# A planner that counts the exclusion of VectorE and GpSimd on SBUF, in a two-layer decoder trunk

## The chip, the core and the metric

The kernel runs on one NeuronCore of a Trainium2 chip. Five engines work side by side, each through its own instructions in order: TensorE (PE, matrix products; PEld in the profile is its weight loading), VectorE (DVE), ScalarE (ACT), GpSimd (POOL) and SyncE (SP, which here starts all DMA transfers). They wait for each other through semaphores. The metric is the device time of one execution in microseconds; the time before is the median of three runs, 1509.18 us (1507.07 to 1511.28).

## The reference

A decoder trunk of two layers on 512 tokens of width 1024, in float32. In each layer:

```
h = rmsnorm(x, g_pre_mix);  proj = h @ w_in          # split into queries, keys, values of four head groups
o_a = top-k sparse attention (an indexer scores the keys, 128 are kept per token)
o_b = forgetting attention (logits plus differences of cumulated log gates)
o_c = differential attention (probs[:, 0] - lam * probs[:, 1], then a norm)
o_d = sliding-window attention with sinks
x = x + rmsnorm(concat(o_a, o_b, o_c, o_d) @ w_out, g_post_mix)
h = rmsnorm(x, g_pre_mlp)
x = x + rmsnorm(square(relu(h @ w_up)) @ w_down, g_post_mlp)      # inner width 4096
x = x + sigmoid(x @ w_ple_gate) * (p_i @ w_ple_proj)
```

Queries and keys of groups a, c and d and of the indexer are rotated (rope).

## The kernel before, in words

Each large product is made of three products of float32r halves: a value is split into a high half (a rounded copy) and a low half (the value less the high half), and `mm3` (line 466) sums high x high, high x low and low x high in PSUM. So every weight tile of 128x1024 that SP loads (`wload`, line 448) costs a copy `whi` on ACT or DVE and a subtraction `wlo` on DVE or POOL, and every activation tile costs a copy (`hth`, or an R, V or P tile) and a subtraction (`htl` and the like). A layer goes through the norm and the rope tables, the head tiles (`head_tile`, line 628: a projection, evacuated from one of two `ps_mm` banks by DVE, rotated by products with the `tab` tiles), the values, the indexer and its top-k (`topk`, line 765, all on DVE), the four attentions, the split of their outputs (`mix_split`, line 779, tiles O), the output projection, 32 tiles of the MLP's first product and four groups of its second, and the gate. `add_normed` (line 526) adds a normed half to x: R<-P,ss,R on DVE, after a small power on POOL. Attention c (line 880) combines two probability tiles on DVE: Z<-Z,s,Z.

The program is not issued as it is written. Class `Plan` records every instruction with its reads and writes, `schedule` (line 290) plays the whole program through once with a cost for each instruction (`price`, line 246) and a table of delays between engines (`SEEN`, line 113), and `emit` (line 417, with line 429 the one line of nearly all rows of the profile) issues the instructions in the order of the planned start times. That order is the program of each engine, and also settles which tile takes which buffer. At each step the engine with the earliest possible start takes the ready instruction of smallest `prio`, which is the place in the written program plus a shift of its step.

Some instructions are recorded with two forms (`either`, line 166): `wlo`, the splits of SBUF tiles, the rope products, the products with a gain, and the copies to a high half. For these `sooner_elsewhere` (line 399) compares the engines: for each, the start it could have, plus the cost of the ready fixed instructions ahead of it, plus the instruction's cost there, plus a bias on DVE. The bias is set by step (lines 1248 to 1261): 4000 ns for v1 and aqk, 2500 for dq, bqk and cqk, 2000 for the output projection, 1500 for va and vc, 1000 for d, 600 for the gains at the start, iq, topk, mix and b, 500 for the MLP, 300 for ik, dk and a, 0 for index and c. If the other engine is better, the form of this one is dropped for good.

In `price`, a DVE instruction of n columns costs n x 1.0417 + 69 ns (n x 0.52 + 69 for a copy, tensor_scalar or memset not read from PSUM, and 61 more with a per-partition operand or a second operation), and a two-input one on POOL n x 2.1 + 147. No cost depends on what the other engine is doing.

Of the kernel before, what the change touches and what calls it, by code (L numbers as in the profile page):

```python
# [134 lines left out]
class Plan:  # L135
# [110 lines left out]
    def price(self, eng, fn, a, k, outs, ins):  # L246
# [25 lines left out]
            return (470.0 if k.get("op") == ALU.pow else n * 2.1 + 147), 0.0  # L272
        return n * 0.833 + 244, 0.0

    @contextmanager
    def after(self, i):

        old, self.held = self.held, i
        yield
        self.held = old  # L280
# [9 lines left out]
    def schedule(self):  # L290
        ops = self.ops
        for i, o in enumerate(ops):
            o.left, o.open = len(o.deps), dict(o.alts) if o.alts else None
            for d in o.deps:
                ops[d].succ.append(i)
            for e in o.alts or (o.eng,):
                o.ready[e] = 0.0
        engines = ("PE", "DVE", "ACT", "POOL", "SP")
        now = dict.fromkeys(engines, 0.0)
        future = {e: [] for e in engines}  # L300
        avail = {e: [] for e in engines}
        dma, now["SP"] = 0.0, 560.0
        table = None
        waiting, live, last, queue = {}, {}, {}, {}

        def push(i):
            for e, r in ops[i].ready.items():
                heapq.heappush(future[e], (r, ops[i].prio, i))

        def after(q, eng, end):  # L310
            for e, r in q.ready.items():
                q.ready[e] = max(r, end if eng == e == "ACT" else end + SEEN[eng, e])

        def grant(t, slot):
            t.granted, t.slot = True, slot
            for i in waiting.pop(t, ()):
                o = ops[i]
                o.left -= 1
                for eng, end in t.freed:
                    after(o, eng, end)  # L320
                if o.left == 0:
                    push(i)

        for tag, (bufs, pool, tiles) in self.tags.items():
            queue[tag] = list(reversed([t for t in tiles if t.ops]))
        for o in ops:
            for t in o.tiles:
                t.granted = t.tag is None or t.tag == "dram"
                t.freed, t.ends = (), {}
        for i, o in enumerate(ops):  # L330
            for t in o.tiles:
                if not t.granted:
                    waiting.setdefault(t, []).append(i)
                    o.left += 1
            if o.left == 0:
                push(i)
        for tag, (bufs, pool, tiles) in self.tags.items():
            for slot in range(bufs):
                if queue[tag]:
                    grant(queue[tag].pop(), slot)  # L340
        order = []
        while True:
            best = None
            for e in engines:
                f, v = future[e], avail[e]
                while f and (f[0][0] <= now[e] or ops[f[0][2]].done):
                    _, p, i = heapq.heappop(f)
                    heapq.heappush(v, (p, i))
                while v and ops[v[0][1]].done:
                    heapq.heappop(v)  # L350
                s = now[e] if v else f[0][0] if f else None
                if s is not None and (best is None or s < best[0]):
                    best = (s, e)
            if best is None:
                break
            s, e = best
            now[e] = max(now[e], s)
            f, v = future[e], avail[e]
            while f and f[0][0] <= s:
                _, p, i = heapq.heappop(f)  # L360
                heapq.heappush(v, (p, i))
            _, i = heapq.heappop(v)
            o = ops[i]
            if o.done or self.sooner_elsewhere(o, e, s, now, avail):
                continue
            o.start, o.done = s, True
            if o.alts:
                o.eng = e
                o.fn, o.a, o.k, o.cost, o.size = o.open[e]
            cost = o.cost  # L370
            if e == "PE" and s < COLD:
                cost *= 2
            if e == "ACT" and o.table and o.table != table:
                cost, table = cost + 1283, o.table
            now[e] = s + cost
            if e == "SP":
                dma = max(dma, s + cost + 650) + o.size
                o.end = dma
            else:
                o.end = now[e]  # L380
            order.append(i)
            for j in o.succ:
                q = ops[j]
                q.left -= 1
                after(q, e, o.end)
                if q.left == 0:
                    push(j)
            for t in o.tiles:
                t.ops -= 1
                t.ends[e] = max(t.ends.get(e, 0.0), o.end)  # L390
                if t.ops == 0 and t.tag is not None and t.tag != "dram" and queue[t.tag]:
                    n = queue[t.tag].pop()
                    n.freed = tuple(t.ends.items())
                    grant(n, t.slot)
        assert len(order) == len(ops), f"{len(ops) - len(order)} instructions never became ready"
        self.total = max(o.end for o in ops)
        return order

    def sooner_elsewhere(self, o, e, s, now, avail):
        if not o.open or len(o.open) < 2:  # L400
            return False
        best = None
        for g, c in o.open.items():
            t = s if g == e else max(now[g], o.ready[g])
            if g != e:
                t += sum(self.ops[i].cost for p, i in avail[g] if p < o.prio and not self.ops[i].done
                         and not self.ops[i].alts)
            t += c[3] + o.bias.get(g, 0.0)
            if best is None or t < best[0]:
                best = (t, g)  # L410
        if best[1] != e:
            del o.open[e]
            del o.ready[e]
            return True
        return False
# [952 lines left out]
```

## Time and profile before

| | |
|---|---|
| median of three runs | 1509.18 us (1507.07 to 1511.28) |
| the profiled execution | 1507.25 us, its span 1505.5 us |
| TensorE's granted clock over the span | 0.987 of full speed |
| instructions in the span | 19889 |
| busy: PE, DVE, ACT, POOL | 1445.8, 908.8, 661.1, 376.7 us |
| HBM read and written | 127.38 and 5.24 MB |

The span is from the first to the last instruction of the profiled execution. A group of rows gives its form as out<-in with buffer numbers left out, the number of instructions, their busy time in us, the mean in ns, and the idle time of the engine before them with what ended it. Matmuls overlap, so a PE that is busy is not necessarily at its peak. An instruction on DVE is counted from its start to the end of its last write, and the next one may start some 0.1 us before that.

### The profile page before, as it was taken

How to read it: one execution, taken by the hardware profiler on the slowest of the kernel's cores; microseconds unless marked ns; L12 is line 12 of the kernel's file. 1: busy time of each engine (PE TensorE's matmuls, PEld its weight loads, DVE VectorE, ACT ScalarE, POOL GpSimd, SP SyncE). 2: the span in 40 equal slices, each digit the busy share in tenths (PEclk: the TensorE clock that was granted, in tenths of full speed). 3: DMA queues.
4: the chain of work that ended last, by engine and by line, in shares of the span. 5: the costliest groups of instructions: out<-in, count | busy, mean ns of one | idle time of the engine just before them, and what ended most of it. 6: DMA issues, size and time to landing. Idle time of an engine off the chain costs nothing. (4 is left out here: it accounts for less than half of the span.)

```text
span 1505.5 us, 19889 instructions
## 1 busy us (share of the span) xinstructions
PE 1445.8 (96%) x7476; PEld 1173.3 (78%) x7476; DVE 908.8 (60%) x1789; ACT 661.1 (44%) x1299; POOL 376.7 (25%) x291
## 2 busy tenths in 40 slices
PE   6999998999999999999999999889999999999998
PEld 6967776778888888887789678577788888888877
DVE  7689998756424333335666999986553243433463
ACT  4266656745323223233344665666543341322321
POOL 5564556342000000002145636563310000000020
PEclk8899999999999999999999999999999999999999
DMA  4321122223222222221332211123132222222221
GB/s 160 100 86 57 57 78 98 78 84 112 99 90 93 98 98 88 94 98 56 122 118 71 74 55 64 64 64 120 52 131 98 99 88 94 98 98 90 92 77 63
DMA packets 44624, 133.91 MB, mean 89 GB/s; under 512 B 6896, under 2 KB 8176, under 8 KB 44528
## 3 DMA queue, kind: packets, MB, share of 16 engines
q1 hardware_dynamic: 44528, 132.64, 26.7%
q8 instruction: 59, 0.97, 0.3%
q14 instruction: 37, 0.30, 0.1%
HBM read 127.38 MB, written 5.24 MB: 88 GB/s over the span
## 5 line engine op out<-in xcount | busy, mean ns | idle before, releaser
L429 DVE TENSOR_TENSOR wlo<-wst,whi 128x1024 fp32r<-128x1024 f32 x150 | 184.2, 1228 | 355.6 <-ACT whi L429 355.4
L429 ACT ACTIVATE whi<-wst 128x1024 fp32r<-128x1024 f32 (+1 forms) x212 | 222.7, 1051 | 397.0 <-PE ps_tp L429 202.1
L429 POOL TENSOR_TENSOR wlo<-wst,whi 128x1024 fp32r<-128x1024 f32 (+1 forms) x70 | 168.5, 2410 | 164.2 <-ACT whi L429 155.8
L429 PE MATMUL ps_sc<-htl,whi 128*128 128x512 f32 (+1 forms) x544 | 208.5, 384 | 1.1 <-DVE htl L429 1.1
L429 PE MATMUL ps_sc<-hth,whi 128*128 128x512 f32 (+1 forms) x544 | 207.6, 383 | 0.3 <-ACT hth L429 0.3
L429 PE MATMUL ps_sc<-hth,wlo 128*128 128x512 f32 (+1 forms) x544 | 206.5, 380 | 0.0
L429 POOL TENSOR_SCALAR ss<-ss,eps 128x1 f32<-128x1 f32 x8 | 3.7, 473 | 637.1 <-ACT Z L429 637.1
L429 PE MATMUL ps_mm<-hth,whi 128*128 128x512 f32 (+1 forms) x400 | 148.3, 372 | 9.6 <-DVE R L429 9.2
L429 PE MATMUL ps_mm<-htl,whi 128*128 128x512 f32 (+1 forms) x400 | 148.1, 371 | 1.8 <-DVE htl L429 1.8
L429 PE MATMUL ps_mm<-hth,wlo 128*128 128x512 f32 (+1 forms) x400 | 146.2, 366 | 0.0
L429 PE MATMUL ps_mm<-whi,htl 128*128 128x512 f32 (+2 forms) x344 | 121.1, 353 | 5.6 <-DVE htl L429 5.6
L429 PE MATMUL ps_mm<-whi,hth 128*128 128x512 f32 (+2 forms) x344 | 122.0, 355 | 0.3 <-DVE V L429 0.2
L429 PE MATMUL ps_mm<-wlo,hth 128*128 128x512 f32 (+2 forms) x344 | 120.1, 350 | 0.1
L429 PEld LDWEIGHTS ps_sc<-hth,whi 128*128 128x128 f32 x544 | 102.0, 188 | 23.0 <-ACT hth L429 0.5
L429 PEld LDWEIGHTS ps_sc<-htl,whi 128*128 128x128 f32 x544 | 102.2, 188 | 22.4 <-DVE htl L429 1.5
L429 PEld LDWEIGHTS ps_sc<-hth,wlo 128*128 128x128 f32 x544 | 102.3, 188 | 21.9
L429 ACT ACTIVATE Z<-Z,m 128x256 f32<-128x256 f32 (+3 forms) x160 | 86.2, 541 | 39.4 <-DVE m L429 38.7
L429 PE MATMUL ps_tp<-whi,V 128*128 128x512 f32 x256 | 96.4, 394 | 0.0
L429 PE MATMUL ps_mm<-whi,V 128*128 128x512 f32 x256 | 96.4, 394 | 0.0
L429 PEld LDWEIGHTS ps_mm<-hth,whi 128*128 128x128 f32 x400 | 77.8, 195 | 20.6 <-issue 11.5
L429 POOL TENSOR_TENSOR R<-R,R 128x512 fp32r<-128x512 f32 (+1 forms) x58 | 76.6, 1321 | 59.1 <-ACT R L429 46.0
L429 PEld LDWEIGHTS ps_mm<-htl,whi 128*128 128x128 f32 x400 | 78.0, 195 | 13.1 <-issue 3.0
(213 smaller groups left out, 2957.4 us busy)
## 6 DMA issues: line engine op xcount, KB each, us to landing
wst<-in_wu SPq DMA_DIRECT2D x64, 512.0 KB, 3.2
wst<-in_wd SPq DMA_DIRECT2D x64, 512.0 KB, 3.2
wst<-in_wq SPq DMA_DIRECT2D x40, 512.0 KB, 3.5
wst<-in_wo SPq DMA_DIRECT2D x16, 512.0 KB, 3.3
wst<-in_wg SPq DMA_DIRECT2D x16, 512.0 KB, 3.2
R<-in_x SPq DMA_DIRECT2D x16, 256.0 KB, 3.6
Z<-in_g SPq DMA_DIRECT2D x16, 256.0 KB, 3.6
wst<-in_wv SPq DMA_DIRECT2D x8, 512.0 KB, 3.2
```

The source lines that it names most:

```text
L429: r = getattr(getattr(nc, eng), fn)(*[res(v) for v in o.a], **{n: res(v) for n, v in o.k.items()})
```

## The change

The planner gets a notion of one shared port between DVE and POOL. A new method `shared` says which DVE instructions take it: those whose operands all lie in SBUF and that either read two tiles of more than 64 columns or are a `tensor_copy` or `tensor_scalar`. Every POOL instruction takes it. `schedule` keeps the time at which the port comes free from either engine; a DVE instruction that takes the port is lengthened by what is left of POOL's, and a POOL instruction by what is left of DVE's. `sooner_elsewhere` gets the same times, and puts the possible start on POOL, or on DVE for an instruction that takes the port, no earlier than the other engine's end. Instructions, costs, biases, shifts and buffers stay as they are.

```diff
+    def shared(self, fn, a):
+
+
+        ins = [v for v in a[1:] if isinstance(v, View) and v.free() > 64]
+        if any(self.psum(v) for v in a if isinstance(v, View)):
+            return False
+        return len(ins) > 1 or fn[1] in ("tensor_copy", "tensor_scalar")
...
+        port = {"DVE": 0.0, "POOL": 0.0}
...
-            if o.done or self.sooner_elsewhere(o, e, s, now, avail):
+            if o.done or self.sooner_elsewhere(o, e, s, now, avail, port):
                 continue
...
             if e == "ACT" and o.table and o.table != table:
                 cost, table = cost + 1283, o.table
+            if e == "DVE" and self.shared(o.fn, o.a):
+                cost += max(0.0, port["POOL"] - s)
+                port["DVE"] = s + cost
+            if e == "POOL":
+                cost += max(0.0, port["DVE"] - s)
+                port["POOL"] = s + cost
             now[e] = s + cost
...
-    def sooner_elsewhere(self, o, e, s, now, avail):
+    def sooner_elsewhere(self, o, e, s, now, avail, port):
...
+            if g == "POOL" or g == "DVE" and self.shared(c[0], c[1]):
+                t = max(t, port["DVE" if g == "POOL" else "POOL"])
             t += c[3] + o.bias.get(g, 0.0)
```

## Rows read from the trace of the kernel before

**Rows 1.** The page's busy time of each engine, share of the span and instructions.

```profile
PE 1445.8 (96%) x7476; PEld 1173.3 (78%) x7476; DVE 908.8 (60%) x1789; ACT 661.1 (44%) x1299; POOL 376.7 (25%) x291
```

**Rows 2.** Windows of 50 us: busy us per engine (instructions), PE clock, DMA share, GB/s.

```profile
200.00:250.00 50.00, 41.97 (x282) 30.81 (x281) 48.81 (x152) 33.45 (x93) 26.31 (x16) 1.00 0.21 69
...
400.00:450.00 50.00, 50.00 (x218) 40.44 (x217) 14.30 (x14) 15.29 (x19) 0.00 (x0) 1.00 0.28 95
...
700.00:750.00 50.00, 44.17 (x197) 34.61 (x195) 31.23 (x35) 17.38 (x26) 10.57 (x10) 0.97 0.27 91
...
950.00:1000.00 50.00, 42.74 (x280) 32.95 (x278) 45.83 (x118) 33.75 (x86) 29.25 (x20) 0.97 0.20 64
```

**Rows 3.** PE's waits over the whole span: us in total, times, longest us.

```profile
PE ps_tp L429 <- DVE Z L429: 9.7, 11, 1.6
...
PE ps_mm L429 <- DVE R L429: 9.2, 2, 7.9
...
PE ps_sc L429 <- DVE R L429: 8.2, 8, 2.6
...
PE ps_mm L429 <- DVE htl L429: 7.4, 3, 2.8
```

**Rows 4.** Groups of DVE instructions by form.

```profile
L429 DVE TENSOR_TENSOR R<-R,tab 128x512 f32<-128x512 f32 x13 | 19.7, 1517 | 0.2
...
L429 DVE TENSOR_TENSOR X<-R,Z 128x512 f32<-128x512 f32 x24 | 15.8, 686 | 4.6 <-DMA Z<-in_g 4.3 <-DVE R L429 0.2
...
L429 DVE TENSOR_TENSOR R<-R,R 128x512 f32<-128x512 f32 x11 | 15.1, 1372 | 0.2
...
L429 DVE SCALAR_TENSOR_TENSOR Z<-Z,s,Z 128x384 f32<-128x384 f32 x8 | 12.6, 1616 | 0.1
...
L429 DVE TENSOR_TENSOR htl<-O,hth 128x512 fp32r<-128x512 f32 x8 | 12.4, 1566 | 0.1
```

**Rows 5.** Timeline at 217 us: start us, us, engine, form, count, idle before.

```profile
217.30 2.37 POOL L429 TENSOR_TENSOR wlo<-wst,whi 128x1024 fp32r<-128x1024 f32 x1
...
217.58 4.06 DVE L429 SCALAR_TENSOR_TENSOR Z<-Z,s,Z 128x384 f32<-128x384 f32 x2
...
220.24 0.52 PE L429 MATMUL ps_tp<-ident,Z 128*128 128x128 f32 x3 [1.61 <-DVE Z L429]
...
221.79 0.52 PE L429 MATMUL ps_tp<-ident,Z 128*128 128x128 f32 x3 [0.80 <-DVE Z L429]
```

**Rows 6.** Timeline at 265 us.

```profile
265.37 5.03 POOL L429 TENSOR_TENSOR htl<-O,hth 128x512 fp32r<-128x512 f32 x3 [4.05 <-PE ps_mm L429]
...
267.51 3.44 DVE L429 TENSOR_TENSOR htl<-O,hth 128x512 fp32r<-128x512 f32 x2
...
271.00 0.49 PE L429 MATMUL ps_mm<-whi,htl 128*128 128x512 f32 x1 [2.79 <-DVE htl L429]
```

**Rows 7.** Timeline at 710 us.

```profile
710.02 2.35 POOL L429 TENSOR_TENSOR wlo<-wst,whi 128x1024 fp32r<-128x1024 f32 x1
...
710.08 3.49 DVE L429 SCALAR_TENSOR_TENSOR R<-P,ss,R 128x512 f32<-128x512 f32 x2 [0.80 <-POOL ss L429]
...
713.06 0.63 PE L429 MATMUL ps_sc<-ident,R 128*128 128x128 f32 x4 [2.57 <-DVE R L429]
```

**Rows 8.** Timeline at 30 us: DVE, POOL, PE.

```profile
29.51 4.67 DVE L429 SCALAR_TENSOR_TENSOR Z<-Z,Z 128x512 f32<-128x512 f32 x4
...
30.41 2.62 POOL L429 TENSOR_TENSOR wlo<-wst,whi 128x1024 fp32r<-128x1024 f32 x1 [3.60 <-ACT whi L429]
...
40.83 0.55 PE L429 MATMUL ps_mm<-hth,whi 128*128 128x256 f32 x1 [7.92 <-DVE R L429]
```

**Rows 9.** POOL: one group by form, and two rows of its timeline.

```profile
L429 POOL TENSOR_TENSOR R<-R,tab 128x512 f32<-128x512 f32 x33 | 43.7, 1335 | 29.4 <-DVE R L429 29.4
...
36.60 1.52 POOL L429 TENSOR_TENSOR tab<-Z,X 128x512 f32<-128x512 f32 x1 [3.58 <-ACT Z L429]
...
807.44 1.29 POOL L429 TENSOR_TENSOR R<-R,R 128x512 fp32r<-128x512 f32 x1 [2.07 <-ACT R L429]
```

## The prediction

> **What bounds the kernel now.** I read the page's busy table first. PE is busy for 1445.8 us of the span of 1505.5 us [rows 1], so at most 59.7 us of this kernel are time in which PE has nothing at all. A change that touches only VectorE (DVE) and GpSimd (POOL) can win its time there and nowhere else. The windows of 50 us say where those holes lie [rows 2]: PE is busy for 50.00 of 50 us in the MLP (400 to 450 us, POOL at 0.00), but for 41.97 in 200 to 250 us, 44.17 in 700 to 750 us and 42.74 in 950 to 1000 us. In 200 to 250 us DVE is at 48.81 of 50: there DVE is the bound, and PE waits for it. Then I asked PE's waits who ends its idle time [rows 3]: DVE every time, above all DVE Z before a transpose (9.7 us, 11 times), DVE R (9.2 us and 8.2 us) and DVE htl (7.4 us).
>
> **Are those waits collisions of DVE and POOL?** The groups of DVE by form give the size of the effect [rows 4]. A product of two SBUF tiles of 128x512 takes 686 ns when left alone (X<-R,Z). The same size takes 1517 ns as R<-R,tab (13 times), 1372 ns as R<-R,R (11 times), 1566 ns as htl<-O,hth (8 times). The excess is 13 x 0.83 + 11 x 0.69 + 8 x 0.88 = 25 us of DVE time in three groups. Z<-Z,s,Z with only 384 columns takes 1616 ns (8 times), at least 8 x 0.93 = 7 us more. The timelines show what the excess is. At 217.30 us POOL starts a wlo of 2.37 us, and two DVE Z<-Z,s,Z that start at 217.58 us need 4.06 us together; PE sits idle for 1.61 us and then 0.80 us for exactly these [rows 5]. At 265.37 us POOL runs three htl, DVE's two htl take 3.44 us, and PE idles 2.79 us [rows 6]. At 710.02 us POOL starts a wlo 0.06 us ahead of the two R<-P,ss,R of add_normed, which need 3.49 us; PE idles 2.57 us [rows 7]. In each case the planner put a PE instruction where its input would have been ready if the two engines did not exclude each other.
>
> **The change, part by part.** Nothing is computed differently and no instruction is added or removed. The planner's clock now charges a wait to a POOL instruction that meets a counted DVE one, and the reverse; the choice between POOL and DVE sees the same wait. So there are two effects: some of the flexible instructions change engine, and the order on every engine, PE, ACT and SP's loads included, is re-derived from the new clock.
>
> *Engine choice.* In the planner's prices (lines 246 to 272) a 512-column subtraction costs 602 on DVE and 1222 on POOL, a 1024-column wlo 1136 and 2297. DVE also carries the step's bias. When POOL is running, DVE no longer wins by starting earlier, because it too starts at POOL's end: from then DVE wins only where the bias is under 620 (512 columns) or 1161 (wlo). When DVE is in a counted instruction, POOL loses its head start likewise. So the small-bias steps lean to DVE (ik and dk 300, iq and mix 600, MLP 500), the large-bias ones (v1, bqk, cqk, dq, aqk, out) to POOL. In the MLP nothing moves: POOL is at 0.00 there already.
>
> Now each hole, with the two ends of what it can give.
> - *The mix split* (bias 600): three htl on POOL against two on DVE. Put on DVE alone, the five need 5 x 0.69 = 3.4 us in place of 5.03 us on POOL. The hole is 2.79 us in layer 0 [rows 6], and PE's three waits for htl are 7.4 us with none over 2.8 us [rows 3], so layer 1 has up to as much: between 0 and 5.6 us; I take half, 2.8, since the copies to hth still come first.
> - *The layer's end* (MLP bias 500): a wlo that meets add_normed goes to DVE behind it if the planner sees add_normed start first, and stays if the wlo is first. The trace has the two 0.06 us apart, so it can fall either way; DVE R before ps_sc holds 8.2 us (8 waits). Between 0 and 8.2; I take 2.5, one of the two big holes.
> - *The Z waits in the third head group's attention*: the colliding POOL work belongs to steps of bias 1500 and 4000 and stays on POOL. What can change is PE's order: knowing that Z is late, the planner can put matmuls of the next projections ahead of these transposes. Between 0 and 9.7; I take half, 4.9.
> - *The start*: PE idles 7.92 us until 40.83 us [rows 8]. Four Z<-Z,Z take 4.67 us there, with a wlo on POOL from 30.41 us for 2.62 us; undisturbed they would take at most 4 x 0.69, so 1.9 us is collision. That wlo may stay or go to DVE, where it would stand in the same chain that PE waits for: 0 to 1.9; I take 0.
> - *The price of the move.* Flexible instructions that go to POOL in the large-bias steps come 1.335 us long in place of 0.69 [rows 4, 9], and PE order loses its fit to some waits that it met before. No row shows this sum; between 0 and the rival's 9.6 us below. I take 2, nearest to the rows of the MLP, where 0 moves.
>
> Sum: 2.8 + 2.5 + 4.9 + 0 - 2 = 8.2 us. The profiled execution took 1507.25 us, its span 1505.5 us, so 1.75 us lie around the span; it is 1.9 us under the median of 1509.18. 1507.25 - 8.2 = 1499.0, and set to the median 1501.0 us. If all holes closed and nothing were paid, 5.6 + 8.2 + 9.7 + 1.9 = 25.4 us would go: 1484 us.
>
> **Rival one: the holes move and do not close** (1509 us). In 200 to 250 us DVE is busy 48.81 of 50 us [rows 2]; a PE that skips ahead there finds itself waiting for the same DVE a little later, and the layer's end is a chain (statistics, add_normed, transposes) with no spare PE work but the gate's matmuls. POOL's work in the attention steps is not moved, so DVE's lost time stays. For it: the largest collisions sit in large-bias steps. Against it: PE has a queue of projections in 200 to 250 us, and the mix split is plainly helped. The change would also do less than it says in that two-input instructions of 64 columns or fewer are not counted. The Trainium skill, in Perfetto Trace Analysis, section Optimizing Scalar/DVE Operations, says that the two engines share an SBUF port, so that moving work from one to the other might not help; by that sentence alone the engine flips would give nothing, and this rival's time would be the result. The trace agrees that they collide [rows 4], and does not show that a better order gains nothing.
>
> **Rival two: DVE becomes the queue at the start of each layer** (slower, 1514 to 1519 us). There the biases are 300 and 600, and DVE evacuates PSUM for the head tiles. POOL now runs 14 flexible 512-column instructions there, seven per layer, from the tab at 36.60 us to the R<-R,R at 807.44 us [rows 9]. If the new rule gives them to DVE, each puts 0.69 us in front of an evacuation for which PE holds its two ps_mm banks, and the index scores, the top-k and the last attention follow by as much: 14 x 0.69 = 9.6 us, 1518.8 us; 1514 us if half of it is hidden. It decides as soon as DVE has no idle time left in these windows. For it: PE's longest single wait, 7.92 us, is for a DVE R at this very place [rows 8]. Against it: DVE's own work there shrinks by the collisions that end, some 0.8 us each [rows 4].
>
> **How the numbers follow.** Two measurements of this kernel can be told apart at about 0.3%, 4.5 us. The forecast (under 1504.6 us) has 0.48: the mechanism is visible at five holes, and only a third of the 25.4 us is claimed. Rival one has 0.24, rival two 0.28: any re-derived order of 19889 instructions can lose what the old one met by luck. The likeliest case's own range is 1487 to 1504.5; with both rivals, and leaving a tenth at either side, 1487 to 1517.
>
> **What would show it.** Right: the mean of htl<-O,hth on DVE falls from 1566 ns towards 690 and PE's wait for it from 7.4 us to under 3; PE waits for DVE Z fall by half; PE busy per window rises to 44 or more in 200 to 250 us. Rival one: the groups of DVE keep their means and PE's idle total stays near 60 us. Rival two: POOL's counts of R fall at 36 to 70 and 780 to 810 us, DVE's rise, and PE's first waits grow. What would make me wrong altogether: a MLP in which POOL appears, or PE's busy time falling below 49.9 of 50 us there.

## The result and the profile after

The changed kernel takes 1482.58 us (median of 4 runs, 1479.35 to 1484.59), the kernel before 1508.12 us on the same chip (4 runs, 1506.11 to 1511.28). The ratio is 0.983, with an interval of 0.980 to 0.985: 25.5 us are gone, where 8.2 us were forecast. The time lies below the range, whose lower end was 1487. That 25.5 is also the "all holes closed" sum of the prediction (25.4) is a coincidence, as the terms show further down. The span fell by the same amount, from 1505.5 to 1480.0 us. The line of the operations is now L446 (L443 for attention's scores) in place of L429 (L426).

The page's busy time of each engine, kernel after, stands against [rows 1]:

```profile
PE 1436.8 (97%) x7476; PEld 1170.2 (79%) x7476; DVE 889.9 (60%) x1804; ACT 667.2 (45%) x1300; POOL 348.3 (24%) x275
```

PE's idle time is span less busy: 59.7 us before, 43.2 us now, so 16.5 us. But PE's busy time fell too, by 9.0 us for the same 7476 matmuls. 16.5 + 9.0 = 25.5. The prediction had no term for the second.

The windows of 50 us, kernel after (columns as in [rows 2]; the first one was not among those rows):

```profile
0.00:50.00 50.00, 35.42 (x225) 33.20 (x226) 36.69 (x71) 20.81 (x38) 16.47 (x25) 0.83 0.44 143
200.00:250.00 50.00, 46.95 (x333) 37.37 (x333) 46.16 (x147) 33.73 (x91) 33.30 (x21) 1.00 0.29 95
400.00:450.00 50.00, 50.00 (x217) 40.51 (x217) 12.84 (x13) 15.85 (x20) 0.00 (x0) 1.00 0.28 95
700.00:750.00 50.00, 50.00 (x234) 40.82 (x233) 34.89 (x42) 23.09 (x39) 11.65 (x15) 1.00 0.39 126
950.00:1000.00 50.00, 44.73 (x310) 35.43 (x308) 44.46 (x126) 36.40 (x85) 27.71 (x18) 1.00 0.26 87
```

The MLP (400 to 450) is as it was. The attention windows hold 46.95 us of PE work in place of 41.97 and 44.73 in place of 42.74, and in 700 to 750 us PE has no idle time left (44.17 before). At the start, this row of the kernel before shows what moved:

```profile
0.00:50.00 50.00, 34.70 (x216) 32.62 (x217) 39.03 (x66) 20.07 (x38) 31.56 (x32) 0.80 0.45 151
```

POOL went from 31.56 to 16.47 us there: of the seven instructions that rival two counted in layer 0's start, four did go to DVE (three tab products and one R<-R,tab), and some wlo with them. PE's busy time in this window did not fall, 35.42 us for 34.70. In the plan of the changed kernel 85 flexible instructions have another engine (26 went from POOL to DVE, 10 from DVE to POOL, 49 changed between ACT and DVE).

PE's waits over the span, kernel after, against [rows 3]:

```profile
PE ps_mm L446 <- DVE R L446: 10.7, 3, 6.4
PE ps_tp L446 <- DVE Z L446: 6.1, 10, 1.1
PE ps_sc L443 <- DVE m L446: 3.9, 7, 1.7
PE ps_sc L446 <- ACT hth L446: 3.7, 2, 2.0
...
PE ps_sc L446 <- DVE htl L446: 1.8, 2, 0.9
...
PE ps_mm L446 <- DVE htl L446: 0.2, 1, 0.2
```

The wait of ps_sc for DVE R, 8.2 us before, has no row any more, and the one of ps_mm for htl fell from 7.4 to 0.2 us. Z fell from 9.7 to 6.1. New is the wait for ACT's hth (0.3 us before).

Did the collisions go? The groups of DVE by form, kernel after, against [rows 4]:

```profile
L446 DVE SCALAR_TENSOR_TENSOR R<-P,ss,R 128x512 f32<-128x512 f32 x32 | 29.0, 949 | 6.5 <-POOL ss L446 6.5
...
L446 DVE TENSOR_TENSOR R<-R,tab 128x512 f32<-128x512 f32 x12 | 14.1, 1175 | 1.4 <-POOL tab L446 1.2
L446 DVE TENSOR_TENSOR R<-R,R 128x512 f32<-128x512 f32 x12 | 12.5, 1042 | 0.2
...
L446 DVE TENSOR_TENSOR htl<-O,hth 128x512 fp32r<-128x512 f32 x8 | 8.5, 1082 | 1.4 <-ACT hth L446 1.4
...
L446 DVE SCALAR_TENSOR_TENSOR Z<-Z,s,Z 128x384 f32<-128x384 f32 x8 | 6.8, 892 | 0.0
```

Some did: Z<-Z,s,Z of 384 columns from 1616 to 892 ns (in all four widths together from 31.7 to 25.0 us), htl<-O,hth from 1566 to 1082, R<-R,R from 1372 to 1042. None is at the 686 ns of a product left alone, and the layer's end, R<-P,ss,R, is worse: 949 ns in place of 878. Yet this is the place whose PE wait vanished. The timeline of layer 0's end, kernel after, answers to [rows 7]:

```profile
704.26 3.55 DVE L446 SCALAR_TENSOR_TENSOR R<-P,ss,R 128x512 f32<-128x512 f32 x2
...
704.46 2.79 POOL L446 TENSOR_TENSOR wlo<-wst,whi 128x1024 fp32r<-128x1024 f32 x1 [0.85 <-ACT whi L446]
...
705.68 0.39 PE L446 MATMUL ps_tp<-whi,R 128*128 128x512 f32 x1
...
705.91 0.39 PE L446 MATMUL ps_mm<-whi,hth 128*128 128x512 f32 x1
...
707.77 0.39 PE L446 MATMUL ps_mm<-whi,htl 128*128 128x512 f32 x1
...
708.00 0.60 PE L446 MATMUL ps_sc<-ident,R 128*128 128x128 f32 x4
```

A wlo collides with the pair of R as before, for 3.55 us in place of 3.49. But PE now does two things ahead of the transposes: the last products of the MLP's second matrix (ps_tp, the last one at 705.68) and nine matmuls of the gate on hth and htl (705.91 to 707.77). The transposes start at 708.00 with no idle time before them. In the kernel before, the same ps_tp products stood behind the transposes, and PE went on with them only at 713.45, after its wait of 2.57 us:

```profile
713.45 0.48 PE L429 MATMUL ps_tp<-whi,R 128*128 128x512 f32 x1
```

So the transposes now stand behind other work, as a planner that expects R late would put them.

**Why PE's busy time fell.** After some holes the granted clock falls. The timeline of PE at the second hole of layer 0's end, kernel before:

```profile
722.27 1.04 PE L429 MATMUL ps_sc<-ident,R 128*128 128x128 f32 x4 [2.55 <-DVE R L429]
722.97 0.77 PE L429 MATMUL ps_mm<-whi,hth 128*128 128x512 f32 x1
...
727.12 0.40 PE L429 MATMUL ps_mm<-whi,htl 128*128 128x512 f32 x1
```

And windows of the same kernel there (PE's busy time third, the granted clock third from the right):

```profile
720.00:721.00 1.00, 0.00 (x0) 0.00 (x0) 1.00 (x1) 0.00 (x1) 1.00 (x1) 1.00 0.00 0
...
723.00:724.00 1.00, 1.00 (x6) 0.82 (x5) 0.94 (x2) 0.60 (x1) 0.00 (x0) 0.50 0.90 348
...
720.00:730.00 10.00, 7.73 (x31) 6.45 (x32) 5.78 (x6) 3.08 (x5) 1.57 (x1) 0.83 0.32 105
```

PE was idle for 2.55 us; then the clock stood at 0.50 (1.2 GHz), and a matmul that takes 0.40 us took 0.77. The hole cost 2.55 us of idle time and then 10 x (1 - 0.83) = 1.7 us of slow matmuls. After 100 us the kernel before has five windows of 10 us at 0.83 (from 110, 270, 720, 960 and 1010 us); the kernel after has two within its matmul stream, from 120 and 270 us. In windows of 1 us, PE's busy time times one minus the granted clock adds up to 15.4 us before and 8.8 us after. So 6.6 of the 9.0 us are the clock by this reading; the other 2.4 us I can't place.

Not every hole is followed by such a stretch. The one of 2.57 us that ends at 713.06 [rows 7] is as long as the one at 722 us, and the clock behind it stays at 1.00:

```profile
714.00:716.00 2.00, 2.00 (x12) 1.69 (x11) 1.91 (x3) 0.92 (x2) 0.00 (x0) 1.00 0.70 242
```

And in the kernel after, where the clock falls at 273 us, no hole in the ten us ahead is longer than 0.61 us. What decides between these cases no run here shows.

### The profile page after: what moved, and what is told of

Read it like the earlier page. It is cut to its first block, busy times and chain, and to the rows that moved or that the text cites. A ratio compares the mean times of both kernels' runs of the same rounds, so it can differ in the third digit from the quotient of the medians.

```text
span 1480.0 us, 19870 instructions
## 1 busy us (share of the span) xinstructions
PE 1436.8 (97%) x7476; PEld 1170.2 (79%) x7476; DVE 889.9 (60%) x1804; ACT 667.2 (45%) x1300; POOL 348.3 (24%) x275
## 4 chain that ended last, share of the span: by engine, by line
PE 76%; DVE 16%; ACT 3%; DMA 2%; issue 2%; POOL 1%; SPq 0%; DVEq 0%; ACTq 0%; POOLq 0%
PE ps_mm L446 29%; PE ps_sc L446 26%; PE ps_tp L446 19%; DVE Z L446 4%; DVE S L446 3%; DVE m L446 2%; PE ps_sc L443 2%; DVE P L446 2%; DVE R L446 2%; DVE O L446 1%; ACT Z L446 1%; DMA wst<-in_wu 1%; DVE s L446 1%; DVE wlo L446 1%; DVE htl L446 1%
## 5 line engine op out<-in xcount | busy, mean ns | idle before, releaser
L446 ACT ACTIVATE whi<-wst 128x1024 fp32r<-128x1024 f32 (+1 forms) x217 | 228.1, 1052 | 416.2 <-PE ps_tp L446 202.1
L446 DVE TENSOR_TENSOR wlo<-wst,whi 128x1024 fp32r<-128x1024 f32 x153 | 188.1, 1230 | 360.3 <-ACT whi L446 360.3
L446 PE MATMUL ps_sc<-hth,whi 128*128 128x512 f32 (+1 forms) x544 | 208.3, 383 | 3.7 <-ACT hth L446 3.7
L446 PE MATMUL ps_sc<-htl,whi 128*128 128x512 f32 (+1 forms) x544 | 206.4, 380 | 1.8 <-DVE htl L446 1.8
L446 PE MATMUL ps_sc<-hth,wlo 128*128 128x512 f32 (+1 forms) x544 | 207.7, 382 | 0.0
L446 POOL TENSOR_TENSOR wlo<-wst,whi 128x1024 fp32r<-128x1024 f32 (+1 forms) x67 | 160.4, 2399 | 178.4 <-ACT whi L446 171.7
L446 POOL TENSOR_SCALAR ss<-ss,eps 128x1 f32<-128x1 f32 x8 | 6.6, 840 | 665.5 <-ACT Z L446 665.5
L446 PE MATMUL ps_mm<-hth,whi 128*128 128x512 f32 (+1 forms) x400 | 146.8, 368 | 11.9 <-DVE R L446 10.7
L446 PE MATMUL ps_mm<-hth,wlo 128*128 128x512 f32 (+1 forms) x400 | 146.2, 367 | 0.0
L446 PE MATMUL ps_mm<-htl,whi 128*128 128x512 f32 (+1 forms) x400 | 145.2, 363 | 0.2 <-DVE htl L446 0.2
L446 PE MATMUL ps_mm<-whi,hth 128*128 128x512 f32 (+2 forms) x344 | 120.9, 352 | 2.1 <-DVE O L446 1.2
L446 PEld LDWEIGHTS ps_sc<-hth,whi 128*128 128x128 f32 x544 | 102.0, 188 | 24.7 <-ACT hth L446 4.1
L446 PEld LDWEIGHTS ps_sc<-htl,whi 128*128 128x128 f32 x544 | 102.2, 188 | 24.1 <-DVE htl L446 2.2
L446 PE MATMUL ps_mm<-wlo,hth 128*128 128x512 f32 (+2 forms) x344 | 120.6, 351 | 0.0
L446 PEld LDWEIGHTS ps_sc<-hth,wlo 128*128 128x128 f32 x544 | 102.2, 188 | 22.3
L446 PE MATMUL ps_mm<-whi,htl 128*128 128x512 f32 (+2 forms) x344 | 119.0, 348 | 0.0
L446 ACT ACTIVATE Z<-Z,m 128x256 f32<-128x256 f32 (+3 forms) x160 | 86.2, 540 | 30.6 <-DVE m L446 29.7
L446 PE MATMUL ps_mm<-whi,V 128*128 128x512 f32 x256 | 96.8, 395 | 0.0
L446 PE MATMUL ps_tp<-whi,V 128*128 128x512 f32 x256 | 96.7, 394 | 0.0
L446 PEld LDWEIGHTS ps_mm<-hth,whi 128*128 128x128 f32 x400 | 77.5, 194 | 23.2 <-issue 12.5
L446 PEld LDWEIGHTS ps_mm<-htl,whi 128*128 128x128 f32 x400 | 77.6, 194 | 10.7 <-issue 2.2
L446 PEld LDWEIGHTS ps_mm<-hth,wlo 128*128 128x128 f32 x400 | 77.2, 193 | 10.9 <-issue 2.7
```

The costliest lines, as they stand in the source:

```text
L446: r = getattr(getattr(nc, eng), fn)(*[res(v) for v in o.a], **{n: res(v) for n, v in o.k.items()})
```

## Experiments

Two effects came with the change, other engines for some instructions and another order on all. **Theory:** the order does it, because PE's program steps round inputs that it knows to be late. **Rivals:** the engine flips do it, because they end collisions; or any newly derived order would have hit such a time by luck.

### One effect at a time

In both kernels a first draft of the plan fixes the engine of every flexible instruction, and a second one, with these engines, gives the order. In e1 the draft is made without the new charge and the order with it; in e2 the reverse.

```
+            if self.force and o.alts:
+                o.alts = {self.force[i]: o.alts[self.force[i]]}
...
-            if e == "DVE" and self.shared(o.fn, o.a):
+            if self.port and e == "DVE" and self.shared(o.fn, o.a):
...
+        draft = type(self)(tc, self.t, self.out)
+        draft.plan.port = False
+        draft.record()
+        draft.plan.schedule()
+        plan.force, plan.port = [o.eng for o in draft.plan.ops], True
```

This is e1; in e2 the two flags, False and True, are exchanged.

Expected of e1:

> The engine of every flexible instruction is the one that the kernel before chose; only the order is planned anew, with the charge for the exclusion. Theory A (the order is what pays: PE's program now has its instructions where DVE's results really come): at least two thirds of the 25.5 us, 1483 to 1492 us, and PE's waits for DVE R before ps_sc under 2 us although R<-P,ss,R on DVE still collides. Theory B (the 85 changed engines pay, by fewer collisions): 1500 to 1509 us. Theory C (luck of a new order): anything between 1485 and 1520 us.

Expected of e2:

> The engine of every flexible instruction is the one that the changed kernel chose; the order is planned with the old clock, without the charge. Theory A: little, 1500 to 1509 us, with PE waits for DVE R and DVE Z as in the kernel before (8 and 10 us). Theory B: 1482 to 1492 us and an excess of DVE as low as in the changed kernel. Theory C: anything between 1485 and 1520 us.

Order alone: 1489.67 us, ratio 0.988 (0.986 to 0.990), so 18.6 us of gain. Choice alone: 1503.09 us, ratio 0.997 (0.996 to 0.998), 5.2 us. Together 23.8 of the 25.5 us, and the order has most of it, as theory A had it for both. The page's busy time and two PE waits of e1:

```profile
PE 1436.8 (97%) x7476; PEld 1173.0 (79%) x7476; DVE 891.9 (60%) x1789; ACT 660.9 (44%) x1299; POOL 379.1 (25%) x291
```

```profile
PE ps_mm L448 <- DVE R L448: 12.2, 2, 9.7
...
PE ps_tp L448 <- DVE Z L448: 4.8, 8, 1.2
```

Engine counts are as before (DVE 1789, POOL 291), and there is no wait of ps_sc for DVE R left. R<-P,ss,R has a mean of 881 ns there, before 878. So the hole at the layer's end closes with the collisions still there. PE's waits of e2, with the flips and the old clock:

```profile
PE ps_tp L448 <- DVE Z L448: 10.5, 7, 3.3
...
PE ps_sc L448 <- DVE R L448: 7.3, 9, 2.2
PE ps_mm L448 <- DVE htl L448: 3.0, 5, 0.7
```

Only htl fell (7.4 to 3.0); Z and R before ps_sc hardly moved. The Trainium skill, in Perfetto Trace Analysis, section Optimizing Scalar/DVE Operations, says that moving work between these two engines might not help as they share an SBUF port. The run with all flips, the 49 between ACT and DVE among them, gained 5.2 of the 25.5 us.

### Which engine's order?

In e13 the four engines DVE, ACT, POOL and SP keep the order and the engines of before, and PE's order alone is planned anew with the charge; in e14 PE keeps its order and the other four are planned anew.

```
+        seq = {e: [i for i in self.fixed if ops[i].eng == e] for e in self.kept}
+        at = dict.fromkeys(seq, 0)
...
+                if e in seq and seq[e][at[e]] != i:
+                    continue
...
+        plan.fixed = draft.plan.schedule()
+        plan.kept = ("DVE", "ACT", "POOL", "SP")
```

This is e13; in e14 `plan.kept` is ("PE",).

Expected of e13:

> Engines of the kernel before, and the order of the kernel before on DVE, ACT, GpSimd and SP; PE's order alone is planned anew, with the charge. If PE's program is where the order pays: at least two thirds of what the order alone gave (18.6 us), 1487 to 1496 us. If the other engines' orders pay: 1503 to 1512 us.

Expected of e14:

> The converse: engines of the kernel before and PE's order of the kernel before; the other four engines' orders are planned anew, with the charge. If PE's program is where the order pays: 1503 to 1515 us. If the other engines' orders pay: 1487 to 1496 us.

PE's order alone: 1498.14 us, ratio 0.994 (0.992 to 0.996), a gain of 9.8 us. That is less than I expected. The rest alone: 1525.23 us, ratio 1.012 (1.009 to 1.014), a loss of 17.3 us, more than expected. So the order's 18.6 us are no sum of the two. PE's waits of e13:

```profile
PE ps_mm L458 <- DVE R L458: 12.5, 5, 10.4
PE ps_tp L458 <- DVE Z L458: 10.1, 8, 2.8
```

and of e14:

```profile
PE ps_tp L458 <- DVE Z L458: 9.6, 8, 1.9
PE ps_sc L458 <- DVE R L458: 8.4, 7, 2.5
PE ps_mm L458 <- DVE whi L458: 8.0, 1, 8.0
PE ps_mm L458 <- POOL wlo L458: 5.2, 1, 5.2
```

Two things separate here. The layer's end (ps_sc for DVE R) is gone in e13 and at 8.4 us in e14: that hole is closed by PE's order. The Z waits stay near 10 us in both, while they fell in e1 (4.8) and in the changed kernel (6.1). And e14's new waits for whi and wlo, 13.2 us at the start of layer 0, show one way in which a half plan loses: DVE and POOL made other splits of the weights first, and PE's old order asks for these first. The wait of ps_sc for DVE m rose there too, from 3.7 to 11.0 us.

### How much is luck?

A plan of some 19,900 instructions jumps when anything in it moves. To see by how much, I shifted all the delays between engines in the planner's tables by -10, +10 and +25 ns, in both kernels, and timed the pairs.

```
-                q.ready[e] = max(r, end if eng == e == "ACT" else end + SEEN[eng, e])
+                q.ready[e] = max(r, end if eng == e == "ACT" else end + SEEN[eng, e] - 10)
```

Expected of e3 (before, -10 ns):

> The kernel before with every delay between engines in the planner's table 10 ns shorter: a new order with no better idea of the two engines. Theories A and B: within 0.5% of the kernel before, 1501 to 1516 us. Theory C: over 0.7% away from it, either way.

Expected of e4 (after, -10 ns):

> The changed kernel with the same 10 ns taken from every delay. Theories A and B: within 0.5% of the changed kernel, 1475 to 1490 us. Theory C: most of the gain can go, 1490 to 1510 us.

Expected of e5 (before, +10 ns):

> The kernel before with 10 ns added to every delay in the planner's table. If a planner that counts the exclusion gives better orders as a rule, this kernel stays at 1495 us or above. If the gain was luck of one order, it can land at 1480 to 1490 us like the changed kernel.

Expected of e6 (after, +10 ns):

> The changed kernel with 10 ns added to every delay. As a rule: at least 5 us under its twin of the kernel before. Luck: as far above it as below, over the three pairs of twins.

Expected of e7 (before, +25 ns):

> The kernel before with 25 ns added to every delay. As a rule: 1495 us or above. Luck: 1480 to 1490 us possible.

Expected of e8 (after, +25 ns):

> The changed kernel with 25 ns added to every delay. As a rule: at least 5 us under its twin of the kernel before. Luck: as far above it as below.

| shift of delays | without the charge | with it | gain |
|---|---|---|---|
| 0 | 1508.12 | 1482.58 | 25.5 |
| -10 ns | 1501.51 | 1495.77 | 5.7 |
| +10 ns | 1527.52 | 1501.52 | 26.0 |
| +25 ns | 1509.61 | 1503.65 | 6.0 |

The charge gains in every pair, 15.8 us on average; with gains from 5.7 to 26.0 us, four pairs leave that average loose. And 10 ns in a table move one kernel by 6.6 us down or 19.4 us up and the other by 13.2 or 18.9 us up: e4 came out where its expectation had put luck (1490 to 1510 us), while the pairs of e5 to e8 came out as a rule would have it. Of four orders with the charge, the one of the change is the best. By the average of the pairs, some 10 of its 25.5 us belong to this one order.

Which holes does the charge close in every order, and which only in some? PE's waits in us, in all the kernels of the trunk:

| kernels | ps_sc for DVE R (layer's end) | ps_tp for DVE Z | ps_mm for DVE htl |
|---|---|---|---|
| PE's order without the charge: before, e2, e3, e5, e7, e12, e14 | 8.2, 7.3, 8.3, 3.1, 6.1, 3.0, 8.4 | 9.7, 10.5, 5.7, 9.2, 3.1, 18.8, 9.6 | 7.4, 3.0, 1.8, 0.6, 1.8, 1.4, 2.5 |
| PE's order with it: after, e1, e13, e4, e6, e8, e10, e11 | 0, 0, 0, 0, 0, 2.2, 0, 0 | 6.1, 4.8, 10.1, 3.1, 6.2, 0.5, 4.7, 4.3 | 0.2, 0.2, 2.9, 0.8, 0.2, 0.9, 0, 0.2 |

The layer's end is closed in seven of eight plans that give PE's order the charge, and in none of the others, though e12, with other settings, has only small waits left there (none over 0.4 us). For Z the two rows overlap, and the kernel before with its delays shifted (e3, e7) lost 4.0 and 6.6 us of that wait without any charge. The big holes for htl at the mix split were gone in e3 and e5 too. So the charge is shown as the cause for the layer's end, and not for the other two.

Where do 13 us come from with -10 ns? The largest part is at the start, in the timeline of e4:

```profile
28.42 3.69 DVE L446 SCALAR_TENSOR_TENSOR Z<-Z,Z 128x512 f32<-128x512 f32 x6
...
28.45 8.07 POOL L446 TENSOR_TENSOR wlo<-wst,whi 128x1024 fp32r<-128x1024 f32 x1 [4.47 <-ACT whi L446]
...
33.90 0.43 DVE L446 TENSOR_SCALAR Z<-Z 128x512 f32<-128x512 f32 x1
...
39.50 0.86 ACT L446 ACTIVATE whi<-wst 128x792 fp32r<-128x792 f32 x1 [11.13 <-DMA wst<-in_wv]
...
46.98 0.55 PE L446 MATMUL ps_mm<-hth,whi 128*128 128x256 f32 x1 [17.30 <-DVE R L446]
```

One wlo on POOL takes 8.07 us in place of some 2.4, while DVE runs a series of products that the planner counts, to 34.33 us; the wlo ends 2.2 us behind that. The buffer wst comes free late, the next load, whi and wlo follow, and behind these come POOL's tab products, for which DVE waits 9.24 us. PE's longest wait is 17.30 us, against 7.92 in [rows 8] and 6.36 and 2.80 in the kernel after: 8.1 of the 15.1 us between the two profiled spans (1495.1 and 1480.0). The planner's rule lets POOL go as soon as DVE's instruction of that moment ends; here it went after the series.

### The exclusion by itself

Is that how the two engines meet? e9 is a kernel with nothing of the model in it: one POOL sum of 128x1024, started by ACT soon after the first of 12 DVE instructions of 128x512. The series is of four kinds, each run twice: free (each reads the same two tiles), a chain (each reads the one before), tensor_scalar on one tile, and free ones mixed with a max of one tile. Its output is not the reference's. The code of the free kind, without its loops over kinds:

```
+nc.vector.tensor_tensor(d[0], c[:, :512], b[:, :512], op=ALU.add)
+nc.scalar.activation(y[:, :512], d[0], AF.Copy)
+nc.gpsimd.tensor_tensor(c, y, b, op=ALU.add)
+for i in range(1, 13):
...
+    nc.vector.scalar_tensor_tensor(d[i], a[:, :512], 0.5, b[:, :512], op0=ALU.mult, op1=ALU.add)
```

Expected of e9:

> No part of the trunk: one SBUF product of 128x1024 on GpSimd meets a series of twelve 128x512 instructions on DVE, which starts about 1.5 us before it, in four kinds, each twice. Alone the GpSimd instruction takes about 2.4 us. If the port is handed over after each DVE instruction, as the changed planner has it, GpSimd waits for at most one of them (under 0.7 us, 3.1 us in all) in every kind, and one DVE instruction in the series is some 2.4 us longer. If DVE keeps the port while its instructions follow each other without a gap, GpSimd takes up to 8 us beside twelve independent ones (two SBUF inputs, or one at double rate), and about 2.5 to 3 us where the series is a chain or every second instruction reads one tile.

The timeline of e9, the POOL sum alone, then the same series twice (the lines of other series are left out):

```profile
5.37 2.34 POOL L30 TENSOR_TENSOR c<-a,b 128x1024 f32<-128x1024 f32 x1 [4.92 <-DMA b<-in_x]
...
8.35 9.45 DVE L38 SCALAR_TENSOR_TENSOR d<-a,b 128x512 f32<-128x512 f32 x12
9.30 2.53 POOL L35 TENSOR_TENSOR c<-y,b 128x1024 f32<-128x1024 f32 x1 [1.60 <-ACT y L34]
...
45.91 7.30 DVE L38 SCALAR_TENSOR_TENSOR d<-a,b 128x512 f32<-128x512 f32 x12
...
46.73 8.68 POOL L35 TENSOR_TENSOR c<-y,b 128x1024 f32<-128x1024 f32 x1 [7.26 <-ACT y L34]
```

The first time POOL's record is only 0.2 us longer than alone, and DVE pays: 9.45 us in place of 7.30. The second time DVE pays nothing, and POOL's record is 8.68 us long, which is the rest of DVE's series (to 53.21) and then its own 2.2 us. So one side does wait for whole instructions of the other. The Trainium skill, in SBUF — State Buffer, section Who interferes with whom, calls the port pair that the two share an exclusive lock. The trace agrees for these two-input instructions. But the side that waits need not be next: POOL can be passed over by a whole series. That happened in one of the eight meetings. In the others POOL was let in at once, as the changed planner has it: 2.53 us here, 2.78 us both times beside a chain, 2.46 beside tensor_scalar, and 2.34 in the mixed series, where one DVE instruction took 2.50 us in place of 0.68. Which way a free series goes, e9 doesn't explain. The code is the same, but POOL's record starts 0.95 us into the series the first time and 0.82 us the second, and no run held that moment fixed.

### A better plan

If the charge makes the planner's clock truer, then its planned end should serve to choose its settings. In e10 the biases and shifts of the changed kernel are those with the smallest planned end that a search over them found; e11 has those of a second search; e12 puts e10's settings into the kernel before.

```
-    shifts = dict(topk=1500)
-    biases = dict(v1=4000, dk=300, ik=300, iq=600, dq=2500, va=1500, bqk=2500, a=300, mix=600, index=0, aqk=4000,
-                  topk=600, b=600, vc=1500, c=0, d=1000, cqk=2500)
+    shifts = dict(topk=1000)
+    biases = dict(v1=0, dk=4000, ik=300, iq=600, dq=1000, va=4000, bqk=1000, a=1500, mix=600,
+                  index=1000, aqk=1500, topk=1500, b=4000, vc=1000, c=0, d=0, cqk=1000)
...
-    table_shift = 100
+    table_shift = 0
...
-    out_bias = 2000.0
-    mlp_bias = 500.0
+    out_bias = 4000.0
+    mlp_bias = 0.0
...
-    gain_bias = 600.0
+    gain_bias = 4000.0
...
-    w_shift = -50
+    w_shift = -100
```

The settings of e11, against those of e10:

```
-    shifts = dict(topk=1000)
+    shifts = dict(topk=2500)
+    biases = dict(v1=2500, dk=1000, ik=600, iq=300, dq=2500, va=600, bqk=4000, a=0, mix=1500,
+                  index=4000, aqk=4000, topk=2500, b=600, vc=4000, c=300, d=2500, cqk=2500)
...
-    table_shift = 0
+    table_shift = 50
...
-    out_bias = 4000.0
+    out_bias = 1500.0
...
-    gain_bias = 4000.0
+    gain_bias = 300.0
```

Expected of e10:

> The changed kernel with biases and shifts that give the smallest end in the changed planner's own clock, over some 200 trials. If that clock is now true enough to choose by: under 1478 us, faster than the changed kernel. If the orders differ by luck alone: 1482 to 1505 us, the range of the changed kernel and its shaken twins.

Expected of e11:

> A second set from another series of some 200 trials, with the same planned end as the first. Clock true enough: under 1478 us. Luck: 1482 to 1505 us.

Expected of e12:

> The first set's biases and shifts in the planner of the kernel before, without the charge. If the settings alone were better: as fast as their twin with the charge. If the charge is what makes an order true: at least 10 us over that twin.

e10: 1458.68 us, ratio 0.967 (0.966 to 0.969), 23.9 us under the changed kernel. e11: 1459.50 us, ratio 0.967 (0.965 to 0.969). e12: 1522.88 us, ratio 1.010 (1.008 to 1.011). The 64.2 us between e12 and e10 are not the worth of the charge alone, since the settings were chosen for the one and not for the other. No run has settings that were searched for by the old clock, which would be the fair twin.

Whether the charged clock is the truer one can be read from the plans themselves. The planned end of each kernel (in the clock by which its order was made) beside its measured time, in us:

| charged clock | planned | measured | old clock | planned | measured |
|---|---|---|---|---|---|
| e10 | 1401.9 | 1458.68 | before | 1390.1 | 1508.12 |
| e11 | 1401.9 | 1459.50 | e3 | 1390.2 | 1501.51 |
| after | 1418.4 | 1482.58 | e2 | 1398.0 | 1503.09 |
| e1 | 1424.0 | 1489.67 | e12 | 1398.8 | 1522.88 |
| e4 | 1425.0 | 1495.77 | e5 | 1404.6 | 1527.52 |
| e13 | 1437.6 | 1498.14 | e7 | 1407.0 | 1509.61 |
| e6 | 1439.5 | 1501.52 | | | |
| e8 | 1445.2 | 1503.65 | | | |
| e14 | 1467.8 | 1525.23 | | | |

With the charge the measured times follow the planned ends in order through all nine kernels, 57 to 71 us above them. With the old clock they lie 103 to 124 us above and do not follow: e2 and e12 are 0.8 us apart in the plan and 19.8 us on the chip. (In e3 to e8 the shifted delays are themselves part of the planned end.) This also tells what the spread of the pairs is: the charged clock had put the order of the change ahead of e4, e6 and e8.

The page's busy time of e10, and its two longest PE waits:

```profile
PE 1423.6 (98%) x7476; PEld 1165.5 (80%) x7476; DVE 997.8 (69%) x1986; ACT 508.9 (35%) x1114; POOL 346.4 (24%) x279
```

```profile
PE ps_mm L446 <- DVE R L446: 7.6, 1, 7.6
PE ps_tp L446 <- DVE Z L446: 4.7, 8, 0.8
```

PE's idle time is 1456.6 - 1423.6 = 33.0 us, and in windows of 1 us the clock costs 4.5 us of PE time, none of it after 100 us. DVE takes 182 instructions more than in the kernel after, most of them from ACT, and R<-P,ss,R still has a mean of 881 ns: here too PE steps round collisions that are still there. For comparison, the longest wait of e12:

```profile
PE ps_tp L429 <- DVE Z L429: 18.8, 11, 4.0
```

## Why the prediction was wrong

The direction was right and the size was not: 25.5 us for 8.2. The terms of its sum, by the same rows of PE's waits:

| term | forecast | measured |
|---|---|---|
| mix split (ps_mm for htl at 271.00 and 1010.79 us) | 2.8 | 5.6 (2.79 and 2.82 to none) |
| first matmuls of the MLP (ps_sc for hth and htl), no term | - | -4.1 (1.4 to 5.5) |
| layer's end (ps_sc for DVE R) | 2.5 | 8.2 (8.2 to no row) |
| Z in the attentions | 4.9 | 3.6 (9.7 to 6.1) |
| starts of the layers (ps_mm for DVE R, and for htl at 27.06 us) | 0 | 0.1 (11.0 to 10.9) |
| price of the move, all other idle time | -2 | 3.1 (what is left of 16.5) |
| PE's busy time, no term | - | 9.0 |

**The step that failed first** is the sentence of the opening that such a change "can win its time there and nowhere else", there being PE's idle time. More than a third of the gain, 9.0 us, is PE's busy time. The rows at 722 us show why the two aren't separate: a hole of 2.55 us is followed by matmuls at half clock. A hole that closes can be worth more than its length, though the one at 713 us was not. The windows that the prediction read showed clocks of 0.97 in two places [rows 2], and no use was made of them.

**The layer's end was mis-sized, by its mechanism.** The prediction let it hang on where the wlo goes ("goes to DVE behind it ... and stays if the wlo is first") and took 2.5 of 8.2. The wlo stayed, the collision grew to 3.55 us, and all 8.2 us went, because PE's order put other matmuls between. The prediction had this mechanism, but booked it for Z alone, and rival one named the gate's matmuls as the only spare work there; the last products of the MLP's second matrix were spare as well. e13 shows that PE's order alone is enough there.

**For Z the mechanism is not shown, and the near number is luck.** With PE's order alone (e13) the Z waits stay at 10.1 us. Shorter collisions don't do it either: in e14 the Z<-Z,s,Z of all widths take 23.9 us, less than the 25.0 of the changed kernel, and the waits stay at 9.6 us. They fell where all engines were planned anew, with the charge (e1, after) but also without it (e3, e7). What made them fall stays open; at 3.6 for 4.9 us the number was near.

**The mix split** gave its upper end, 5.6 us. The layer 1 hole that the prediction could only bound is one of 2.82 us at 1010.79 us, and both closed; the third wait for htl that it counted with them, 1.77 us at 27.06, belongs to the start. But htl<-O,hth is at 1082 ns and not near 690, so the collisions there were cut by half, not ended, and a wait for ACT's copies to hth came up at the first matmuls of the MLP (1.63 and 2.04 us). Both holes were gone without the charge in e3 and e5 as well, so this gain can't be put down to it.

**The price of the move** showed no loss: its row, with all other idle time in it, gained 3.1 us. Rival two's move happened in part at the start of layer 0, for four of seven instructions, and hardly in layer 1, and the starts lost nothing, where it priced 4.8 to 9.6 us. Rival one, holes that move, is refuted by the idle total of 43.2 us, which it put near 60.

**The range** had no term for what one order is worth by chance. The four pairs spread from 5.7 to 26.0 us, some 10 us to either side of the 15.8 that the charge gave on average; with such a term the lower end would have stood near 1482 (1508.1 - 25.8). By that average, which four pairs leave loose, the forecast of 8.2 us is about half of what the charge gives, and the rest of the miss is this order.

**Its signs.** The wait for htl fell under 3 us (0.2) and PE's busy time in 200 to 250 us rose over 44 (46.95), as it said. The mean of htl<-O,hth did not come near 690 ns, and the Z waits fell by 3.6 of 9.7 us, not by half.

**Left open:** the 2.4 us of PE's busy time that the clock doesn't account for. In e1 the busy time fell by the same 9.0 us, and the clock's sum by 3.7 only (15.4 to 11.7). In e10 it fell by 22.2 us (1445.8 to 1423.6), and the clock's sum by 10.9. So the clock is a part of the fall and not shown as the whole of it. No run held the clock and changed the holes.

## What to carry to other kernels

Where a list scheduler lays out several engines, a resource that two of them share belongs into its clock even if the collisions can't be avoided: 18.6 of the 25.5 us came from a new order with the engines of before, and the hole that closed most reliably did so because the third engine was given other work for that time. Count an idle hole of the matmul engine at its length plus the slow matmuls behind it, where the windows show any. And before a single order is taken as the worth of a rule, shake a table by a few nanoseconds and time some pairs; ask, too, whether the planned ends follow the measured times. Here they did with the charge, and settings chosen by that clock gave almost as much again (1458.7 us).

## What was not expected

- A GpSimd instruction that waits for the shared port can be passed over by a whole back-to-back series of VectorE's: 8.68 us for 2.34 us of work in e9, and 8.07 us in e4, where it cost PE a wait of 17.30 us. The same series in the same kernel let it in at once the first time (2.53 us), and so did six other series.
- Tiny VectorE instructions feel it too: s<-s,lam on 128x2 went from a mean of 328 to 549 ns (16 instructions), and the charge leaves out anything of 64 columns or fewer. In the kernel after one of them starts at 237.88 us and takes 1.17 us in place of some 0.21; it ends at 239.05, just as the POOL wlo that started at 236.62 (2.42 us) ends at 239.04. What counting them would gain no run tried.
- Shifting all planned delays by 10 ns moves the measured time by up to 19.4 us.
